# One model step of two trunk layers on one NeuronCore: turning v, k and the output rows in fewer, larger steps

## The chip, the cores and the metric

The kernel runs on one core of a Trainium2 chip. Its time is the device time of one execution in microseconds (us), and the kernel before was run three times. One further execution was recorded by the hardware profiler; the rows quoted below come from that one. Engines are called as the profile calls them: PE is TensorE's matmul side and PEld its weight load, DVE is VectorE, ACT is ScalarE, POOL is GpSimd, and SP is SyncE, which here only issues DMA transfers.

## The reference

One inference step of two layers for a prompt of 512 tokens and 8 samples of one token each, in float32, model width 1024. Layer 0 is a short gated convolution beside dilated sliding-window attention. Layer 1 is mean pooling beside retention in 4 heads of width 256. Each layer has a modulated norm, one wide input and one output projection, and a gated residual. A final RMSNorm gives the output rows. The parts that the change touches:

```python
def retention_chunk(state, q, k, v, log_g):
    ...
    scores = jnp.einsum('bihk,bjhk->bhij', q, k) * decay
    inner = jnp.einsum('bhij,bjhv->bihv', scores, v)
    ...
    kd = k * jnp.exp((L - 1.0 - t)[:, None] * log_g[None, :])[None, :, :, None]
    new_state = jnp.exp(L * log_g)[None, :, None, None] * state + jnp.einsum('bjhk,bjhv->bhkv', kd, v)
    return new_state, inner + cross

def odd_layer(x, c, g, aw, ab, w_in, pw, ps, w_out, pool_prev, ret_prev, pos0):
    ...
    o = o * lax.rsqrt(jnp.mean(o * o, axis=-1, keepdims=True) + EPS)
    y_d = o.reshape(Bn, L, W_D).astype(x.dtype) * jax.nn.silu(gd)
    out = jnp.concatenate([y_c, y_d], axis=-1) @ w_out
    return x + gate * out, pool_new, ret_new.astype(x.dtype)
...
    y_prompt = rmsnorm(xp, norm_f)
    y_sample = rmsnorm(xs, norm_f)
```

The outputs also hold the new retention states of the prompt (one 256x256 per head) and of the 8 samples (8 times as many).

## The kernel before

**Layout.** Activations lie features on partitions, tokens along the free axis: 8 tiles of 128 features by 520 columns (512 prompt tokens and 8 samples). A projection streams weight tiles of 128x1024 from HBM in the fixed order of a list. Float32 products are made of three: each operand is split into a rounded high part and a remainder (fp32r), and hi x hi, hi x lo and lo x hi are summed in PSUM. For weights ACT writes the high part (`whi`) and DVE the remainder (`wlo`).

**The stream.** `product` works on one weight tile in 8 k-steps; each is 6 matmuls (three products by two halves of 260 columns or so). After each k-step `advance` issues the splitting and loading of later weight tiles, and `tick` runs what stands in four lists: `at(n, fn)` runs a function n ticks later; `put(fn, after=n)` puts one into a queue of side steps, of which one runs at each tick once its time has come; `put_fill` steps run where no side step is due; `put2` steps run one at every second tick. So whatever PE does besides projections (transposes, states, scores) stands between two k-steps, and each engine works through its instructions in the order in which these functions wrote them. Semaphores between the engines follow from the tiles.

**Memory.** PSUM holds two 2-bank tiles `mm` for the projections and four 1-bank tiles `aux` for side steps. SBUF has rotating buffers `t` (52 of up to 530 columns), `v` (4 of 1024 columns) and `big` (3 of 2048 columns).

**A retention head** (`ret_head`, four times). Products for v (two tiles), k (two), q (two) and the gate (two) stream by. Beside them run:
- `v_turn` (L970): four transposes of one v tile (L973), so that tokens lie on partitions; ACT writes the high part `vh`, DVE the low one. `v_rows` (L1066, transposes L1069): the 8 samples' v rows are turned, copied by ACT (8x256), written to DRAM (`vdr`) a tick later, and read back spread over all partitions by `v_cast` (tiles `vb`, shown as v).
- `k_turn` (L977, transposes L980): four transposes of one k tile, the decay `kd` by DVE (L146, t<-aux,csm), rounding by ACT, and the remainder by DVE (t<-t,t).
- `state` (four steps): 6 matmuls each of `kd` and `vh`/`vl` (aux<-v,t), the new prompt state.
- `state_new`: for each sample ACT decays the state (big<-big) and DVE adds two outer products (L149, big<-v,ksc,big). It is a `put2` step.
- `score`, `weigh`, `state_read`, `sample_out`, `sample_ms`, `norm`, `gate`: the scores, the weighted sums, the samples' outputs, and the RMS scale of both.

For head 0 the first k-steps run before the layer's normalisation factors are there, so its steps are due later (`DV` = 9 and `DK` = 10 ticks).

**The end.** The last projection goes tile by tile (`out_tile`, 8 of them), `gated` (L149, t<-mm,mG,t) adds the residual, and `rows(m, blocks)` turns a tile's 128 features of a block of 128 tokens (transposes L1299), lets ACT sum the squares, and lets DVE multiply by `norm_f` into output rows. The last tile is done in two column halves. `rows_scale(blocks)` adds the squares, takes the root (ACT) and the reciprocal (DVE, L1308), scales the rows, and sends them (DMA at L1315). Five blocks: four of the prompt and the 8 samples.

## Time and profile before

| what | value |
|---|---|
| three runs | 1062.13, 1062.48, 1064.51 us; median 1062.48 |
| the profiled execution | 1062.29 us |
| its span, first to last instruction | 1060.3 us |
| instructions | 21050 |
| moved by DMA | 168.95 MB, mean 159 GB/s |

The span is shorter than the execution's own time by what lies around it, 2.0 us. The page names groups of instructions by line, engine, operation and tiles: `t<-aux,csm` reads the tiles aux and csm and writes a tile t. L140 is the helper for ACT's activation, L146 DVE's two-tensor operation, L149 the operation of scalar and two tensors, L153 tensor by scalar, L157 a load on SP's queue, L160 every matmul. A row of the timeline has the start in us, the duration of a piece (several instructions of a kind back to back are one row with their count), and in brackets how long the engine was idle before and what ended it. In a row of the windows view stand the window, its length, each engine's busy time, the granted clock, the DMA share and the rate.

The groups of DMA issues in the page show the median from issue to landing:

```profile
wraw<-in_w_in_o SPq DMA_DIRECT2D x48, 512.0 KB, 3.7
big<-in_state_ret SPq DMA_DIRECT2D x16, 512.0 KB, 8.0
```

The weights of layer 1 land 3.7 us after their issue, the samples' states 8.0 us.

### The profile page before, as it was taken

The numbers are of one execution on the slowest core, as the hardware profiler recorded it, in microseconds if no ns is written. First come the engines' busy times: TensorE is split into PE (matmuls) and PEld (weight loads), VectorE is DVE, ScalarE is ACT, GpSimd is POOL, SyncE is SP. The second block draws the span as 40 slices with busy tenths as digits, with TensorE's granted clock in tenths as the row PEclk, the third lists the DMA queues.
The fourth block names the chain that finished last, engine by engine and source line by source line (L and its number), as shares of the span: only waits on it lengthen the run. The fifth ranks groups of instructions, "written<-read, shape, count | busy, mean of one in ns | idle before, by whom it ended". The sixth has DMA issues, their size and how long they took to land.

```text
span 1060.3 us, 21050 instructions
## 1 busy us (share of the span) xinstructions
PE 1036.2 (98%) x8682; PEld 991.1 (93%) x8682; DVE 623.1 (59%) x1470; ACT 489.1 (46%) x884; POOL 4.3 (0%) x33
## 2 busy tenths in 40 slices
PE   5999999999999999999999999999999999999996
PEld 3899999999989999999999998999999999999996
DVE  4666676766785444456344486665657576674443
ACT  5666567665654222224233474435444453333333
POOL 0000000000000000000000000000000000000000
PEclk9999999999999999999999999999999999999999
DMA  9576654666536636613744246363826423225322
GB/s 348 209 255 196 184 157 169 173 211 190 142 119 203 196 107 194 199 60 129 240 154 140 100 159 205 103 204 118 261 83 213 159 80 129 80 83 169 100 71 81
DMA packets 82175, 168.95 MB, mean 159 GB/s; under 512 B 7208, under 2 KB 47240, under 8 KB 79000
## 3 DMA queue, kind: packets, MB, share of 16 engines
q1 hardware_dynamic: 81792, 167.09, 48.9%
q8 instruction: 68, 1.11, 0.4%
q10 hardware_dynamic: 288, 0.52, 0.1%
q14 instruction: 27, 0.22, 0.1%
HBM read 149.40 MB, written 18.65 MB: 158 GB/s over the span
## 4 chain that ended last, share of the span: by engine, by line
PE 90%; DVE 5%; ACT 2%; issue 1%; DVEq 0%; ACTq 0%
PE mm L160 74%; PE aux L160 13%; DVE t L146 2%; PE aux L604 1%; ACT t L140 1%; DVE wlo L146 1%; DVE t L149 0%; PE aux L1299 0%; PE aux L518 0%; DVE big L149 0%; PE aux L973 0%; PE aux L980 0%; PE aux L374 0%; ACT md L140 0%; ACT whi L140 0%
## 5 line engine op out<-in xcount | busy, mean ns | idle before, releaser
L160 PE MATMUL mm<-t,whi 128*128 128x256 f32 (+1 forms) x4608 | 759.1, 286 | 1.1 <-DVE zs L143 0.8
L160 PEld LDWEIGHTS mm<-t,whi 128*128 128x128 f32 x4608 | 636.1, 188 | 19.9 <-issue 15.5
L160 PE MATMUL mm<-t,wlo 128*128 128x256 f32 (+2 forms) x2304 | 465.8, 282 | 0.0
L160 PEld LDWEIGHTS mm<-t,wlo 128*128 128x128 f32 x2304 | 358.1, 188 | 0.0
L146 DVE TENSOR_TENSOR wlo<-wraw,whi 128x512 fp32r<-128x512 f32 x288 | 188.4, 683 | 58.1 <-ACT whi L140 57.4
L140 ACT ACTIVATE whi<-wraw 128x1024 fp32r<-128x1024 f32 x144 | 151.6, 1053 | 94.3 <-PE mm L160 58.7
L146 DVE TENSOR_TENSOR t<-t,t 128x520 fp32r<-128x520 f32 (+6 forms) x182 | 119.0, 657 | 99.3 <-ACT t L140 97.7
L140 ACT ACTIVATE t<-t 128x520 fp32r<-128x520 f32 (+3 forms) x116 | 71.0, 616 | 161.8 <-DVE t L149 103.1
L140 ACT ACTIVATE t<-aux 128x512 f32<-128x512 f32 (+7 forms) x156 | 70.9, 464 | 133.3 <-PE aux L160 83.4
L140 ACT ACTIVATE t<-mm 128x512 f32<-128x512 f32 (+2 forms) x116 | 56.3, 507 | 111.3 <-PE mm L160 109.1
L146 DVE TENSOR_TENSOR t<-aux,t 128x384 fp32r<-128x384 f32 (+6 forms) x120 | 58.6, 494 | 42.8 <-ACT t L140 38.0
L160 PE MATMUL aux<-t,t 64*128 64x256 f32 (+6 forms) x384 | 54.0, 324 | 0.0
L160 PE MATMUL aux<-t,v 128*128 128x512 f32 (+2 forms) x224 | 50.0, 325 | 0.0
L160 PEld LDWEIGHTS aux<-t,t 64*128 64x128 f32 (+1 forms) x384 | 41.0, 186 | 4.3
L583 DVE CUSTOM_DVE_ANT_0 t<-aux,t 128x128 f32<-128x128 f32 (+3 forms) x64 | 28.2, 488 | 27.5 <-PE aux L160 27.5
L140 ACT ACT_TABLE_LOAD x32 | 41.1, 1283 | 1.3 <-PEq L1414 0.7
L140 ACT ACTIVATE t<-t,mn 128x128 f32<-128x128 f32 (+3 forms) x64 | 35.4, 554 | 7.9 <-DVE mn L583 7.9
L160 PEld LDWEIGHTS aux<-t,v 128*128 128x128 f32 x224 | 34.8, 188 | 1.8 <-DVE t L146 0.8
L149 DVE SCALAR_TENSOR_TENSOR big<-v,ksc,big 128x256 f32<-128x256 f32 x64 | 27.7, 480 | 11.8 <-ACT big L140 10.4
L143 DVE COPY zs<-mm 128x8 f32<-128x8 f32 x76 | 12.0, 158 | 37.2 <-ACT t L140 31.8
L146 DVE TENSOR_TENSOR t<-mm,t 128x512 f32<-128x512 f32 (+1 forms) x24 | 16.5, 689 | 29.2 <-PE mm L160 21.6
L146 DVE TENSOR_TENSOR gtmp<-mm,mG 128x8 f32<-128x8 f32 x16 | 2.6, 165 | 44.8 <-PE mm L160 44.8
(153 smaller groups left out, 557.7 us busy)
## 6 DMA issues: line engine op xcount, KB each, us to landing
wraw<-in_w_in_e SPq DMA_DIRECT2D x64, 512.0 KB, 4.9
wraw<-in_w_in_o SPq DMA_DIRECT2D x48, 512.0 KB, 3.7
big<-in_ada_e SPq DMA_DIRECT2D x12, 1024.0 KB, 11.8
big<-in_ada_o SPq DMA_DIRECT2D x12, 1024.0 KB, 9.8
wraw<-in_w_out_e SPq DMA_DIRECT2D x16, 512.0 KB, 3.9
big<-in_state_ret SPq DMA_DIRECT2D x16, 512.0 KB, 8.0
out_new_ret_sample<-big SPq DMA_DIRECT2D x16, 512.0 KB, 5.1
wraw<-in_w_out_o SPq DMA_DIRECT2D x16, 512.0 KB, 3.4
```

What stands on the lines that cost most here:

```text
L140: return nc.scalar.activation(out=out, in_=in_, func=func, scale=scale, **kw)
L143: return nc.vector.tensor_copy(out, in_)
L146: return nc.vector.tensor_tensor(out=out, in0=in0, in1=in1, op=op)
L149: return nc.vector.scalar_tensor_tensor(out=out, in0=in0, scalar=scalar, in1=in1, op0=op0, op1=op1)
L160: nc.tensor.matmul(out, lhsT=lhsT, rhs=rhs, start=start, stop=stop)
L583: nc.vector.tensor_tensor_reduce(out=sb, in0=s[:, 0:n], in1=bt[e][:, S - n:S], scale=1.0, scalar=3e38, op0=ALU.add, op1=ALU.min, accum_out=mn,
L604: nc.tensor.transpose(ep[:, c * P:(c + 1) * P], st["E", e][blk[0]][:, blk[1] * P:(blk[1] + 1) * P], ident)
```

## The change

Layer 0: the transposes and sums of the gate's modulation (`ada_fin` with "g") are no step of their own two ticks after, but the first thing in `window_gather`, four ticks after.

Retention heads: both v tiles and the samples' v rows are turned in one step (10 transposes; before, 4, 4 and 2 in three steps). The 8x256 copy stands first on ACT; the low parts follow one and two ticks later. Both k tiles are turned in one step (8 transposes), the first tile's decay in it, the second's a tick later, the low half of each a tick after its decay (`hilo_later`). The states are due one tick later. The samples' squares are summed over partitions in `norm`, beside the prompt's, and `norm` is due three ticks after `sample_out`, where `sample_ms` was.

The end: the full blocks of `rows` share one PSUM tile; in the stream all five blocks are done in one step, three ticks after (before, three blocks at two ticks and two at four). The output rows lie in two `big` tiles, two blocks each, and one `v` tile for the samples. DVE scales even blocks, ACT odd ones, 1024 columns at a time, and one transfer of 512 KB takes a block out (before, two of 256 KB); odd blocks go by ACT's queue. The samples' rows are one transfer.

```diff
@@ -765,15 +765,15 @@
                         windows[b0 + u][:, t, half * 512:(half + 1) * 512], t == 0, t == 1,
                     )
         mdg = ada_mm(ada_g.pop(b0 // 2))
-        put_fill(ada_fin, 0, "g", b0 // 2, mdg, after=2)
...
-        put(window_gather, b0, om, after=4)
-
-    def window_gather(b0, om):
+        put(window_gather, b0, om, mdg, after=4)
+
+    def window_gather(b0, om, mdg):
+        ada_fin(0, "g", b0 // 2, mdg)
...
@@ -967,20 +967,38 @@
         st = {"of": [], "sq": []}
         yD = [None, None]
 
-        def v_turn(i, vf):
-            pt = aux([P, 4, P])
-            for jb in range(4):
-                nc.tensor.transpose(pt[:, jb, :], vf[:, jb * P:(jb + 1) * P], ident)
-            act(st["vh"][:, :, i, :], pt)
-            lo_of(st["vl"][:, :, i, :], pt, st["vh"][:, :, i, :])
-
-        def k_turn(i, kf):
-            pt = aux([P, 4, P])
-            for jb in range(4):
-                nc.tensor.transpose(pt[:, jb, :], kf[:, jb * P:(jb + 1) * P], ident)
+        def turned(parts):
+            out = []
+            for x in parts:
+                pt = aux([P, 4, P])
+                for jb in range(4):
+                    nc.tensor.transpose(pt[:, jb, :], x[:, jb * P:(jb + 1) * P], ident)
+                out.append(pt)
+            return out
+
+        def v_turn(parts):
+
+            pts = turned(parts)
+            pq = aux([NB, 2, P])
+            for i in range(2):
+                nc.tensor.transpose(pq[:, i, :], zs[1][:, 32 + 2 * h + i, :], ident)
+            vt = tt(2 * P, p=NB)
+            act(vt, flat(pq))
+            at(1, load, vdr[h], vt)
+            at(4, v_cast)
+            for i, pt in enumerate(pts):
+                act(st["vh"][:, :, i, :], pt)
+                at(1 + i, lo_of, st["vl"][:, :, i, :], pt, st["vh"][:, :, i, :])
+
+        def k_turn(parts):
+            pts = turned(parts)
+            k_decay(0, pts[0])
+            at(1, k_decay, 1, pts[1])
+
+        def k_decay(i, pt):
             kd = tt(S)
             vtt(p4(kd), pt, csm[:, C_KDEC + 4 * h:C_KDEC + 4 * h + 4].unsqueeze(2).to_broadcast([P, 4, P]), ALU.mult)
-            st["kd", i] = [p4(x) for x in hilo(kd, S)]
+            st["kd", i] = [p4(x) for x in hilo_later(1, kd, S)]
 
...
@@ -1034,7 +1052,8 @@
                     vtt(st["sq"][0], st["sq"][0], sq, ALU.add)
 
         def norm():
-            ms = aux([P, S])
+            st["om"], ms = aux([P, NB]), aux([P, S])
+            mm(st["om"], on_d, st["oq"][:, 0, :], True, True)
             mm(ms, on_d, st["sq"][0], True, True)
...
@@ -1062,15 +1081,6 @@
         def fin(i):
             yhl[2 * h + i] = hilo(yD[i])
 
-
-        def v_rows():
...
-            at(4, v_cast)
 
...
@@ -1120,17 +1130,13 @@
             vtt(oq, oS, oS, ALU.mult)
             vtt(oq[:, 0, :], oq[:, 0, :], oq[:, 1, :], ALU.add)
             st["oS"], st["oq"] = oS, oq
-            put(sample_ms, after=3)
-
-        def sample_ms():
-            st["om"] = aux([P, NB])
-            mm(st["om"], on_d, st["oq"][:, 0, :], True, True)
             st["orr"] = mk(cp, [P, NB], F32, "orr", 2)
-            put(norm, after=1)
+            put(norm, after=3)
 
 
         st["vh"] = t4(dt=F32R).rearrange("p (a i d) -> p a i d", a=4, i=2)
         st["vl"] = t4(dt=F32R).rearrange("p (a i d) -> p a i d", a=4, i=2)
+        vfs, kfs = [], []
         for i in range(2):
...
-            put(v_turn, i, vf, after=DV if h == 0 else 2)
-        put(v_rows, after=DV if h == 0 else 2)
+            vfs.append(vf)
+        put(v_turn, vfs, after=DV if h == 0 else 2)
         for i in range(2):
...
@@ -1152,12 +1158,13 @@
                 act(p2(kf), ps[:, :, 0:H0], ACTF.Copy, scale=1.0 / 16.0)
                 sample_z(1, 24 + 2 * h + i, ps)
             at(1, k_split, i, kf)
-            put(k_turn, i, kf, after=DK if h == 0 else 2)
+            kfs.append(kf)
+        put(k_turn, kfs, after=DK if h == 0 else 2)
         st["ksc"] = mk(cp, [P, 2, NB], F32, "ksc", 2)
         vts(st["ksc"], zs[1][:, 24 + 2 * h:26 + 2 * h, :], 1.0 / 16.0, None, ALU.mult)
         for i in range(2):
             for part in range(2):
-                put(state, i, part, after=5 + (DK if h == 0 else 0))
+                put(state, i, part, after=6 + (DK if h == 0 else 0))
...
@@ -1274,8 +1281,8 @@
     load(o["pool_keep"], a["state_pool"][0, :, 1:15, :])
 
 
-    xo = [[tt(512) for _ in range(2)] for _ in range(4)]
-    xos = [tt(512, p=NB) for _ in range(2)]
+    xo2 = [big().rearrange("p (i d) -> p i d", i=2) for _ in range(2)]
+    xo = [xo2[i // 2][:, i % 2] for i in range(4)] + [t4(p=NB)]
...
@@ -1293,13 +1300,19 @@
 
         hf, c = m // 4, (m % 4) * P
         sq = tt(P)
+        pts = {}
+        full = [i for i in blocks if i < 4]
+        pt = aux([P, len(full), P])
+        for n, i in enumerate(full):
+            pts[i] = pt[:, n, :]
+        if 4 in blocks:
+            pts[4] = aux([NB, P])
+        for i in blocks:
+            nc.tensor.transpose(pts[i], xT[m][:, i * P:min(i * P + P, T)], ident)
         for i in blocks:
             n = P if i < 4 else NB
-            px = aux([n, P])
-            nc.tensor.transpose(px, xT[m][:, i * P:i * P + n], ident)
-            act(sq[0:n], px, ACTF.Square, scale=1.0 / 32.0, accum_out=ss[0:n, i, m:m + 1])
-            dst = xo[i] if i < 4 else xos
-            vtt(dst[hf][:, c:c + P], px, nf[hf][0:n, c:c + P], ALU.mult)
+            act(sq[0:n], pts[i], ACTF.Square, scale=1.0 / 32.0, accum_out=ss[0:n, i, m:m + 1])
+            vtt(xo[i][:, hf * 512 + c:hf * 512 + c + P], pts[i], nf[hf][0:n, c:c + P], ALU.mult)
 
     def rows_scale(blocks):
         i0, i1 = blocks[0], blocks[-1] + 1
@@ -1307,16 +1320,15 @@
         act(rs[:, i0:i1], rs[:, i0:i1], ACTF.Sqrt, bias=eps[:, 0:1])
         nc.vector.reciprocal(rs[:, i0:i1], rs[:, i0:i1])
         for i in blocks:
-            if i < 4:
-                act(xo[i][0], xo[i][0], ACTF.Copy, scale=rs[:, i:i + 1])
-                vts(xo[i][1], xo[i][1], rs[:, i:i + 1], None, ALU.mult)
-                for hf in range(2):
-                    q = nc.scalar if i == 1 else nc.sync
-                    q.dma_start(out=o["y_prompt"][0, i * P:(i + 1) * P, hf * 512:(hf + 1) * 512], in_=xo[i][hf])
+            if i == 4:
+                vts(xo[i], xo[i], rs[0:NB, i:i + 1], None, ALU.mult)
+                load(o["y_sample"].rearrange("b s d -> (b s) d"), xo[i])
+            elif i % 2:
+                act(xo[i], xo[i], ACTF.Copy, scale=rs[:, i:i + 1])
+                nc.scalar.dma_start(out=o["y_prompt"][0, i * P:(i + 1) * P, :], in_=xo[i])
             else:
-                for hf in range(2):
-                    vts(xos[hf], xos[hf], rs[0:NB, i:i + 1], None, ALU.mult)
-                    load(o["y_sample"].rearrange("b s d -> (b s) d")[:, hf * 512:(hf + 1) * 512], xos[hf])
+                vts(xo[i], xo[i], rs[:, i:i + 1], None, ALU.mult)
+                load(o["y_prompt"][0, i * P:(i + 1) * P, :], xo[i])
 
     def res1(m):
         xT[m] = tt()
@@ -1328,8 +1340,7 @@
         at(6, res1, m + 1)
         out_tile(1, m, ps)
         gated(1, m, ps, xT[m])
-        for n, b in ((2, range(3)), (4, range(3, 5))):
-            at(n if m < KT - 2 else n + 2, rows, m, b)
+        at(3 if m < KT - 2 else 5, rows, m, range(5))
 
 
     m = KT - 1
```

The order of instructions on the engines, at three places. First DVE in head 0, from the decay of the first k tile on. Before, t_7695 is the decayed first k tile and t_7698 its low half; big_7573 is the samples' state that takes up the v rows v_7638; t_7755 is the low half of q; t_7779 and t_7782 are the second k tile.

```order
L146 TENSOR_TENSOR t_7695<-aux_7690,csm 128x512
L146 TENSOR_TENSOR t_7698<-t_7695,t_7697 128x512
L149 SCALAR_TENSOR_TENSOR big_7573<-v_7638,ksc_7662,big_7573 128x256 x2
L146 TENSOR_TENSOR wlo_7716<-wraw_7379,whi_7688 128x512
L149 SCALAR_TENSOR_TENSOR big_7573<-v_7638,ksc_7662,big_7573 128x256 x2
L146 TENSOR_TENSOR wlo_7716<-wraw_7379,whi_7688 128x512
L149 SCALAR_TENSOR_TENSOR big_7573<-v_7638,ksc_7662,big_7573 128x256 x4
L146 TENSOR_TENSOR t_7755<-mm_7671,t_7754 128x512
L143 COPY zs_95<-mm_7671 128x8
L146 TENSOR_TENSOR t_7779<-aux_7774,csm 128x512
L146 TENSOR_TENSOR t_7782<-t_7779,t_7781 128x512
```

After, t_7773 and t_7776 are the first k tile, t_7787 and t_7790 the second, big_7566 the state, t_7744 the low half of q.

```order
L149 SCALAR_TENSOR_TENSOR big_7566<-v_7630,ksc_7662,big_7566 128x256 x2
L146 TENSOR_TENSOR wlo_7705<-wraw_7379,whi_7688 128x512
L149 SCALAR_TENSOR_TENSOR big_7566<-v_7630,ksc_7662,big_7566 128x256 x2
L146 TENSOR_TENSOR wlo_7705<-wraw_7379,whi_7688 128x512
L149 SCALAR_TENSOR_TENSOR big_7566<-v_7630,ksc_7662,big_7566 128x256 x4
L146 TENSOR_TENSOR t_7744<-mm_7671,t_7743 128x512
L143 COPY zs_95<-mm_7671 128x8
L146 TENSOR_TENSOR t_7773<-aux_7763,csm 128x512
L146 TENSOR_TENSOR t_7776<-t_7773,t_7775 128x512
L146 TENSOR_TENSOR t_7787<-aux_7768,csm 128x512
L146 TENSOR_TENSOR wlo_7798<-wraw_7452,whi_7761 128x512
L146 TENSOR_TENSOR t_7790<-t_7787,t_7789 128x512
```

The first k tile's two instructions moved from ahead of the samples' state to behind it, q and the copy to zs; the second k tile follows at once.

Second, DVE in head 1, at the same point. Before, t_8448 and t_8451 are the first k tile and its low half, big_8338 is the samples' state, t_8535 the low half of q.

```order
L146 TENSOR_TENSOR t_8448<-aux_8443,csm 128x512
L146 TENSOR_TENSOR t_8451<-t_8448,t_8450 128x512
L149 SCALAR_TENSOR_TENSOR big_8338<-v_8325,ksc_8415,big_8338 128x256 x2
L146 TENSOR_TENSOR wlo_8469<-wraw_8161,whi_8441 128x512
L149 SCALAR_TENSOR_TENSOR big_8338<-v_8325,ksc_8415,big_8338 128x256 x2
L146 TENSOR_TENSOR wlo_8469<-wraw_8161,whi_8441 128x512
L149 SCALAR_TENSOR_TENSOR big_8338<-v_8325,ksc_8415,big_8338 128x256 x4
L146 TENSOR_TENSOR t_8535<-mm_8424,t_8534 128x512
```

After, t_8442 and t_8445 are the first k tile and its low half, t_8457 and t_8460 the second's.

```order
L146 TENSOR_TENSOR t_8442<-aux_8432,csm 128x512
L149 SCALAR_TENSOR_TENSOR big_8338<-v_8319,ksc_8404,big_8338 128x256 x2
L146 TENSOR_TENSOR t_8445<-t_8442,t_8444 128x512
L146 TENSOR_TENSOR t_8457<-aux_8437,csm 128x512
L146 TENSOR_TENSOR wlo_8468<-wraw_8161,whi_8430 128x512
L146 TENSOR_TENSOR t_8460<-t_8457,t_8459 128x512
L149 SCALAR_TENSOR_TENSOR big_8338<-v_8319,ksc_8404,big_8338 128x256 x2
L146 TENSOR_TENSOR wlo_8468<-wraw_8161,whi_8430 128x512
L149 SCALAR_TENSOR_TENSOR big_8338<-v_8319,ksc_8404,big_8338 128x256 x4
```

Two instructions of the state moved in between the first k tile's decay and its low half, and the second k tile stands ahead of the second pair and among the weights' low halves.

Third, ACT at the end of the program, with what each instruction waits for: the last two blocks. Before, the squares of the two blocks (t_12779), the root, the scaling of the first halves, and block 1's two transfers:

```order
L140 ACTIVATE t_12779,ss<-aux_12780 128x128 [waits PE_49]
L140 ACTIVATE t_12779,ss<-aux_12784 128x128 [waits PE_49,Activation_49]
L140 ACTIVATE rs<-rs,eps 128x2 [waits DVE_49]
L140 ACTIVATE t_11640<-t_11640,rs 128x512 [waits DVE_49]
L140 ACTIVATE t_11642<-t_11642,rs 128x512
L1315 DMA out_y_prompt<-t_11642 128x512 [waits DMAHW7_49,Activation_49]
L1315 DMA out_y_prompt<-t_11643 128x512 [waits DMAHW1_49,DVE_49]
```

After, the squares (t_12737), the root, the scaling of one whole block, and its transfer:

```order
L140 ACTIVATE t_12737,ss<-aux_12738 128x128 [waits PE_49]
L140 ACTIVATE t_12737,ss<-aux_12738 128x128 [waits DVE_49]
L140 ACTIVATE rs<-rs,eps 128x2 [waits DVE_49]
L140 ACTIVATE big_11640<-big_11640,rs 128x1024 [waits DVE_49]
L1328 DMA out_y_prompt<-big_11640 128x1024 [waits DMAHW4_49,Activation_49]
```

Both squares read the same PSUM tile now (aux_12738), and the second waits for DVE, where it waited for PE and for ACT itself.

More of the change, by code (lines that the diff above doesn't have):

```diff
@@ L1063, in fin @@
             yhl[2 * h + i] = hilo(yD[i])
-        def v_rows():
-            pq = aux([NB, 2, P])
-            for i in range(2):
-                nc.tensor.transpose(pq[:, i, :], zs[1][:, 32 + 2 * h + i, :], ident)
-            vt = tt(2 * P, p=NB)
-            act(vt, flat(pq))
-            at(1, load, vdr[h], vt)
-            at(4, v_cast)
         def v_cast():
```

## The prediction

> **What bounds the kernel now.** I read the page's busy line and chain first, then the cores' clocks, then PE's waits.
>
> ```profile
> PE 1036.2 (98%) x8682; PEld 991.1 (93%) x8682; DVE 623.1 (59%) x1470; ACT 489.1 (46%) x884; POOL 4.3 (0%) x33
> PE 90%; DVE 5%; ACT 2%; issue 1%; DVEq 0%; ACTq 0%
> core 0: 1060.3 us, clock 0.998
> PE aux L160 <- DMA t<-in_x_t: 9.2, 1, 9.2
> PE aux L348 <- ACT md L140: 3.4, 2, 1.7
> PE aux L160 <- DVE t L146: 2.0, 4, 1.0
> PE mm L160 <- DVE zs L143: 0.8, 2, 0.7
> ```
>
> TensorE works 98% of the span at full granted clock and makes 90% of the chain. Its waits are few: 9.2 us at the start for the input, then 3.4, 2.0 and 0.8 us. So a change elsewhere can gain only where PE stands today, or at the tail behind PE's last work, and it loses where it makes PE stand. Three things can change: what a group of small PE instructions costs, PE's stalls in the four heads, and the tail.
>
> **Groups of transposes.** A side step slips its PE instructions between two k-steps of six matmuls, two steps become one, and I need the price of a group. The next matmul's start misleads; the price is in the whole gap up to the matmuls behind it.
>
> ```profile
> 613.18 0.41 PE L160 MATMUL mm<-t,wlo 128*128 128x256 f32 x2
> 613.43 0.60 PE L973 MATMUL aux<-csm,t 128*128 128x128 f32 x4
> 614.36 0.41 PE L160 MATMUL mm<-t,wlo 128*128 128x256 f32 x2
> 615.10 0.41 PE L160 MATMUL mm<-t,wlo 128*128 128x256 f32 x2
> 620.72 0.40 PE L160 MATMUL mm<-t,wlo 128*128 128x256 f32 x2
> 620.96 0.38 PE L1069 MATMUL aux<-csm,zs 128*8 128x128 f32 x2
> 621.67 0.41 PE L160 MATMUL mm<-t,wlo 128*128 128x256 f32 x2
> ```
>
> 614.36 to 615.10 is a bare k-step: 0.74 us. With four transposes in it, 613.18 to 614.36 takes 1.18, so they cost 0.44. With two, 620.72 to 621.67 takes 0.95, so they cost 0.21. That is 0.105 to 0.11 each and, from 2 x 0.21 against 0.44, between -0.02 and +0.02 for being a group. The change keeps the number of transposes and ends some 27 groups (two in v and one in k of each head, four sample matmuls in norm, four gathers in layer 0, seven in the output rows). I take 0.008 each, **-0.2 us** (bounds -0.5 and +0.5).
>
> **Head 0.** Here PE does stand today.
>
> ```profile
> 637.26 0.87 PE L160 MATMUL aux<-v,t 128*128 128x256 f32 x6
> 637.97 0.64 PE L160 MATMUL mm<-t,whi 128*128 128x256 f32 x4
> 638.68 0.87 PE L160 MATMUL aux<-v,t 128*128 128x256 f32 x6
> 640.21 0.72 PE L160 MATMUL mm<-t,whi 128*128 128x256 f32 x4 [0.66 <-DVE zs L143]
> 641.38 0.50 PE L160 MATMUL aux<-v,t 128*128 128x256 f32 x2 [0.21 <-ACT t L140]
> 642.11 0.74 PE L160 MATMUL aux<-v,t 128*128 128x256 f32 x4 [0.22 <-DVE t L146]
> 642.68 0.53 PE L160 MATMUL mm<-t,whi 128*128 128x256 f32 x3
> ...
> 631.63 0.68 DVE L146 TENSOR_TENSOR t<-aux,csm 128x512 f32<-128x512 f32 x1
> 633.02 0.69 DVE L146 TENSOR_TENSOR t<-t,t 128x512 fp32r<-128x512 f32 x1 [0.70 <-ACT t L140]
> 634.93 0.88 DVE L149 SCALAR_TENSOR_TENSOR big<-v,ksc,big 128x256 f32<-128x256 f32 x2 [1.22 <-ACT big L140]
> 639.91 0.15 DVE L143 COPY zs<-mm 128x8 f32<-128x8 f32 x1
> 639.99 0.68 DVE L146 TENSOR_TENSOR t<-aux,csm 128x512 f32<-128x512 f32 x1
> 641.36 0.69 DVE L146 TENSOR_TENSOR t<-t,t 128x512 fp32r<-128x512 f32 x1 [0.70 <-ACT t L140]
> ...
> 626.35 0.35 ACT L140 ACTIVATE t<-aux 8x256 f32<-8x256 f32 x1
> 629.10 0.85 SPq L157 DMA_DIRECT2D v<-vdr  x2
> ```
>
> A state step takes 0.71 us (637.26 to 637.97), state plus k-step 1.42. From 638.68 to 642.68 stand two states and a k-step, worth 2.13; it took 4.00, so 1.87 us are lost. The cause is DVE's list: kd0 is decayed at 631.63 and split at 633.02, then DVE waits for the sample state's operands, v rows that return from DRAM (629.10, put on its way by the copy at 626.35), and its pair at 634.93, the rest of that chain, zs and kd1 (639.99) all come late.
>
> In the changed kernel the copy stands first in its step, right behind transposes at about 621: it can come 0 to 5.2 us earlier, I take 2.6. The loads of v rows also stand ahead of a weight load that they followed. kd0 no longer stands ahead of the sample state, so the pair can start as soon as DVE is free, where kd0 was: 631.63, or 3.3 earlier. Then zs ends at 640.06 - 3.3 = 636.8 and the 0.66 wait for it goes. **What is late next** is kd0, now behind that chain: decay to 637.4, rounding on ACT (the 0.70 of idle) to 638.1, split to 638.7. PE reaches the first state one k-step later than now, since it is due a tick later, at 637.97; its third matmul, the first to read the low half, wants it at 638.3. PE stands 0.4, and with restart and rounding I take 0.65. The later states find kd1 ready. Head 0: 0.65 - 1.87 = **-1.2 us**. At best nothing stands, -1.87. If the sample state starts at 634.93 as now, kd0 takes kd1's place (split done 642.05), PE stands 642.05 - 638.3 = 3.75 and some 0.3 for restarts: **+2.2**.
>
> **Heads 1 to 3.** Nothing stands here now; kd0's two parts follow each other with a hole.
>
> ```profile
> 692.20 0.68 DVE L146 TENSOR_TENSOR t<-aux,csm 128x512 f32<-128x512 f32 x1
> 693.58 0.69 DVE L146 TENSOR_TENSOR t<-t,t 128x512 fp32r<-128x512 f32 x1 [0.70 <-ACT t L140]
> 694.19 0.88 DVE L149 SCALAR_TENSOR_TENSOR big<-v,ksc,big 128x256 f32<-128x256 f32 x2
> 691.47 0.60 PE L980 MATMUL aux<-csm,t 128*128 128x128 f32 x4
> 694.05 0.87 PE L160 MATMUL aux<-v,t 128*128 128x256 f32 x6
> ```
>
> The split ends at 694.27; PE's third state matmul reads it at 694.35, hardly spared. The changed order puts the sample pair (0.8 from 692.88, so to about 693.7) into the 0.70 hole. It overfills it by 0.1, and the group of eight transposes moves what stands before kd0, so the split ends some 0.2 behind PE's need: 0.25 a head, **+0.8 us** for three (bounds 0 and +2.3, the latter if the pair still waits half a microsecond for its DMA). The weight splits after it come 1.4 us later (two DVE instructions of 0.69 slipped ahead); no row of PE's waits names a weight, so I cost that at nothing, covered by the tiles split ahead; without that cover it would be 1.4 a head.
>
> **At nothing.** Layer 0's gate sums go two ticks later: read only at that layer's output, many products on. In norm the same two matmuls stand in one step, and its results are read after that head. Output rows in the stream: the same squares and multiplies at three ticks instead of two and four, under PE's products, with DVE 59% and ACT 46% busy. If that cover were gone it would be one block's square and multiply, 0.6 us, in each of seven.
>
> **The tail.**
>
> ```profile
> 1053.12 0.28 ACT L140 ACTIVATE t<-aux 128x128 f32<-128x128 f32 x1
> 1053.12 0.69 DVE L146 TENSOR_TENSOR t<-aux,t 128x128 f32<-128x128 f32 x2 [0.82 <-ACT t L140]
> 1054.46 0.88 DVE L153 TENSOR_SCALAR t<-t,rs 128x512 f32<-128x512 f32 x2
> 1055.20 0.83 SPq L1315 DMA_DIRECT2D out_y_prompt<-t  x2
> 1056.20:1058.70 2.50, 0.00 (x0) 0.00 (x0) 0.00 (x0) 0.00 (x0) 0.00 (x0) 0.50 1.04 394
> ```
>
> Now ACT squares the second block at 1053.12 while DVE multiplies the first: two PSUM tiles. With one tile the changed order makes the second square wait for DVE's first multiply, and the second multiply for that square: +0.35, and +0.11 as the first square waits for both transposes. Then a 1024-wide scaling (0.88 for two halves) comes before the first transfer, which now goes after one 512-wide one: first transfer at 1054.46 + 0.46 + 0.77 = 1055.7 against 1055.20, the second, behind ACT, about when the last goes now. From 1056.20 the transfers run at 394 GB/s, 1 MB in 2.66 us, so they are bound by bytes, and four 256 KB pieces or two of 512 KB differ little: I give back 0.1. **+0.4 us** (bounds -0.1, if the start of the transfers doesn't set their end, and +0.6).
>
> [...]
>
> **The sum.** -0.2 - 1.2 + 0.8 + 0.4 = -0.2. The profiled execution took 1062.29 (span 1060.3), so 1062.1; the median of the three runs, 1062.48, stands 0.19 above it: **1062.3**.
>
> **The rivals.**
> - **Slower: kd0 held behind a transfer.** DVE takes its list in order, and the sample pair now stands ahead of kd0's split in each head, and in head 0 ahead of its decay too. If the pair waits for its v rows, the state step waits with it. Price: head 0 +2.2 in place of -1.2, so 1065.7; with +2.3 in the other heads 1067.2. It decides once the pair in head 0 starts after about 633. For it: that pair waited 1.22 us for its operands today. Against: the copy and loads start earlier.
> - **Faster: no stall left.** Head 0 -1.87, other heads 0, groups -0.2, tail between -0.1 and +0.4: 1060.3 to 1060.8. For it: kd0 misses its turn by only 0.2 to 0.4 in my working.
> - **The change doesn't do what it says, the price being per group.** If ending a group saved a whole 0.1, 27 would give -2.7 and 1059.8. Against: 0.44 for four and 0.21 for two.
> - **The clock falls in the long groups.** The window behind PE's last work shows it at 0.50. Ten transposes take 1.1 us; if each of eight long groups brought 3 us at half speed, 8 x 1.5 = +12, so 1074. Against: that window begins over 3 us after PE stopped, and the mean clock is 0.998 with groups of four and six. [...]
>
> **How the numbers follow.** 0.2% is 2.1 us, about what a measurement of this kernel can tell from no change: faster is below 1060.4, slower above 1064.6. Forecast 0.56 (its own range 1061.0 to 1063.8), slower rival 0.16, faster rival 0.22, per group 0.04, clock 0.02. Of the faster rival half falls below 1060.4: 0.11 + 0.04 = 0.15 faster. Slower: 0.16 + 0.02 less 0.02 where kd0 is held only briefly: 0.16. Within: 0.69. The range takes in the better part of the faster rival and head 0's part of the slower one: 1060.0 to 1066.0.
>
> **What would show it.** Right: PE's row at 640.21 loses its wait for zs, and a short wait for DVE's t stands at the first state of each head; in the tail the two squares of the last tile stand 0.7 apart. Wrong: DVE's pair in head 0 starts at 633 or later and PE's waits for DVE's t grow to 4 us or more; or they vanish in all heads; or k-steps with eight or ten transposes take less than 0.74 + 0.1 for each; or a PEclk below 9 in layer 1.

## The result: slower by 1.3%, and the profile after

| kernel | median us | runs us |
|---|---|---|
| before | 1062.48 | 1061.70 to 1064.51 (5) |
| changed | 1077.48 | 1071.94 to 1079.93 (5) |

The ratio is 1.013, with a 95% interval of 1.0114 to 1.0147. The forecast was 1062.3, and its range ended at 1066.0. The profiled execution took 1079.93 with a span of 1078.0, so it is the slowest of the five and 17.7 us of span above the one before. The five runs' mean clocks go from 0.997 (1071.94) to 0.988 (1079.93).

The changed kernel's page, in the order of before:

```profile
PE 1045.0 (97%) x8682; PEld 998.5 (93%) x8682; DVE 621.9 (58%) x1467; ACT 489.2 (45%) x882; POOL 4.3 (0%) x33
PEclk9999999999999999999999999999899999999998
```

Its span and mean granted clock:

```profile
core 0: 1078.0 us, clock 0.988
```

PE's waits (total us, times, longest):

```profile
PE aux L160 <- DVE t L146: 11.8, 6, 3.9
PE aux L160 <- DMA t<-in_x_t: 8.7, 2, 8.4
PE aux L348 <- ACT md L140: 3.1, 2, 1.7
PE mm L160 <- DVE zs L143: 0.2, 1, 0.2
```

PE does the same 8682 matmuls, but its waits for DVE's t went from 2.0 to 11.8 us, and the clock from 0.998 to 0.988. The wait for zs of head 0 went as forecast. To see where the time came in, I compare the start of the same projection's first matmul in the two traces (later minus earlier, us; before's own times in the first row):

```
                  layer 1  head 1  head 2  head 3  pooling  last matmul
before             597.97  664.39  726.54  788.65   850.73      1051.50
changed             +0.21   -0.87   +5.68  +11.61   +17.78       +17.35
```

Head 0, between "layer 1" and "head 1", gained 1.1 us. Heads 1, 2 and 3 lost 6.55, 5.93 and 6.17, together 18.65, and everything behind them hardly moved. Head 1 on PE, DVE, ACT and SP's queue (start, duration, instruction, idle before):

```profile
693.80 0.40 PE L160 MATMUL aux<-v,t 128*128 128x256 f32 x2
698.06 1.23 PE L160 MATMUL aux<-v,t 128*128 128x256 f32 x4 [3.86 <-DVE t L146]
699.08 1.07 PE L160 MATMUL mm<-t,whi 128*128 128x256 f32 x4
...
690.82 0.69 DVE L146 TENSOR_TENSOR t<-aux,csm 128x512 f32<-128x512 f32 x1
696.52 0.88 DVE L149 SCALAR_TENSOR_TENSOR big<-v,ksc,big 128x256 f32<-128x256 f32 x2 [5.02 <-ACT big L140]
697.32 0.69 DVE L146 TENSOR_TENSOR t<-t,t 128x512 fp32r<-128x512 f32 x1
...
695.86 0.63 ACT L140 ACTIVATE big<-big 128x512 f32<-128x512 f32 x1 [3.69 <-DMA big<-in_state_ret]
...
683.81 0.33 SPq L157 DMA_DIRECT2D wraw<-in_w_in_o  x1
684.23 0.85 SPq L157 DMA_DIRECT2D v<-vdr  x2
685.14 1.06 SPq L157 DMA_DIRECT2D big<-in_state_ret  x2
```

Read it from PE backwards. The first state step starts at 693.80, and its third matmul, which needs kd0's low half, starts at 698.06. That half is made by DVE at 697.32, behind the samples' state pair, which stood 5.02 us. The pair waited for ACT's decay of the state, and that for the load, asked for at 685.14 and landed by 695.86, 10.7 us later. In heads 2 and 3 PE stood 2.97 and 3.18 us at the same place, so 10.0 us in all.

The rest is the clock. Quarter microseconds of the windows view in the changed kernel, with the granted clock third from the end:

```profile
694.50:694.75 0.25, 0.00 (x0) 0.00 (x0) 0.00 (x0) 0.00 (x0) 0.00 (x0) 1.00 0.98 348
696.50:696.75 0.25, 0.00 (x0) 0.00 (x0) 0.23 (x1) 0.00 (x0) 0.00 (x0) 1.00 1.03 332
697.00:697.25 0.25, 0.00 (x0) 0.00 (x0) 0.25 (x2) 0.00 (x0) 0.00 (x0) 0.50 1.10 361
703.50:703.75 0.25, 0.25 (x3) 0.25 (x3) 0.00 (x0) 0.25 (x1) 0.00 (x0) 0.50 0.91 377
704.00:704.25 0.25, 0.25 (x4) 0.25 (x4) 0.25 (x1) 0.00 (x0) 0.00 (x0) 1.00 0.57 209
```

The granted clock fell to 0.50 at about 697, 2.8 us after the last matmul ended (694.2), and came back to 1.00 at about 703.8, though PE worked again from 698.06. A k-step and the state step behind it took 2.58 us there (699.08 to 701.66), against 1.42 in the kernel before (694.76 to 696.18). From the first state step to the k-step behind the third, head 1 took 10.26 us (693.80 to 704.06) against 3.56 before (694.05 to 697.61). That is 6.70 more: the 3.86 of standing and 2.84 behind it. In heads 2 and 3, where the clock was at 0.50 for 6.8 us each and PE worked about 6.2 of them, the same stretch took 9.55 and 9.77 us against 3.59 and 3.55, and 2.99 and 3.04 came behind the standing. So 10.0 of standing and 8.9 behind it make 18.9. (By estimate some 0.8 of the 8.9 is not the clock: in e9 below, where the clock held at 1.00 behind a wait of 3.41, the same stretch of head 1, 695.17 to 702.41, took 0.27 more than 3.56 and the wait.) The merged groups give some 0.3 back (heads 1 to 3 gain 0.26 in e1 and 0.34 in e2 below, where PE does not stand), which makes 18.6 against the 18.65 of the table.

### The profile page after: what moved, and what is told of

The parts are those of the page before. It is cut to its first block, busy times and chain, and to the rows that moved or that the text cites. A ratio compares the mean times of both kernels' runs of the same rounds, so it can differ in the third digit from the quotient of the medians.

```text
span 1078.0 us, 21011 instructions
## 1 busy us (share of the span) xinstructions
PE 1045.0 (97%) x8682; PEld 998.5 (93%) x8682; DVE 621.9 (58%) x1467; ACT 489.2 (45%) x882; POOL 4.3 (0%) x33
## 3 DMA queue, kind: packets, MB, share of 16 engines
q8 instruction: 68, 1.11, 0.4%
q10 hardware_dynamic: 288, 1.05, 0.3%
HBM read 149.40 MB, written 18.65 MB: 156 GB/s over the span
## 4 chain that ended last, share of the span: by engine, by line
PE 84%; DVE 6%; DMA 3%; ACT 3%; issue 1%; SPq 0%; ACTq 0%; DVEq 0%
PE mm L160 68%; PE aux L160 13%; DMA big<-in_state_ret 3%; DVE t L146 2%; ACT t L140 2%; PE aux L604 1%; DVE wlo L146 1%; DVE big L149 1%; DVE t L149 0%; DMA qdr<-t 0%; DVE v L146 0%; PE aux L1311 0%; SPq L157 0%; ACT big L140 0%; ACT whi L140 0%
## 5 line engine op out<-in xcount | busy, mean ns | idle before, releaser
L146 DVE TENSOR_TENSOR t<-aux,t 128x384 fp32r<-128x384 f32 (+4 forms) x80 | 47.2, 598 | 33.4 <-ACT t L140 29.4
L160 PE MATMUL aux<-v,t 128*128 128x256 f32 x96 | 19.8, 351 | 10.1 <-DVE t L146 10.0
```

The lines of the kernel that those rows point to most:

```text
L146: return nc.vector.tensor_tensor(out=out, in0=in0, in1=in1, op=op)
L160: nc.tensor.matmul(out, lhsT=lhsT, rhs=rhs, start=start, stop=stop)
```

## The experiments

Theory A: kd0's low half is held on DVE, which takes its list in order, behind a pair that waits for the state's load; the standing then drops the clock. Rivals: B, the long groups of transposes drop the clock; C, the state steps are due too early whatever DVE does first; D and E, other loads make the state's load late; F, the loads wait in SP's queue. All kernels below are the changed one with one edit, unless said otherwise. Each was timed beside the kernel before on the same chip.

**Both k tiles decayed and split at once (e1).**

```diff
             k_decay(0, pts[0])
-            at(1, k_decay, 1, pts[1])
+            k_decay(1, pts[1])
...
-            st["kd", i] = [p4(x) for x in hilo_later(1, kd, S)]
+            st["kd", i] = [p4(x) for x in hilo(kd, S)]
```

> Both k tiles are decayed and split at once in k_turn, so on DVE both low halves stand ahead of the samples' state pair; transposes, state times and loads stay as changed. Theory A (kd0's split is held on DVE behind a pair that waits for the load of the samples' state): PE's waits for DVE's t in heads 1 to 3 (3.9, 3.0 and 3.2 us in the changed kernel) go, the granted clock stays 1.00 there, about 1061.5 us (before 1062.5, less 1.4 of head 0, plus 0.35 of the tail). Rival B (the long groups of eight and ten transposes drop the clock, not the standing): the clock still falls in heads 1 to 3, some 2.7 us each, about 1069. Rival C (the state steps are due too early whatever DVE does first): waits of 2 us and more stay, 1070 or more.

Measured 1060.46 us, 0.9981 of before (0.9970 to 0.9992). DVE in head 1 of e1:

```profile
693.75 0.69 DVE L146 TENSOR_TENSOR t<-t,t 128x512 fp32r<-128x512 f32 x1 [0.70 <-ACT t L140]
696.45 0.88 DVE L149 SCALAR_TENSOR_TENSOR big<-v,ksc,big 128x256 f32<-128x256 f32 x2 [2.01 <-ACT big L140]
```

PE's waits for DVE's t over the whole of e1:

```profile
PE aux L160 <- DVE t L146: 1.8, 3, 1.0
```

The pair is as late as in the changed kernel (696.45 against 696.52) and DVE still stands 2.01 us for it. But all four k instructions are through by then, PE does not stand, and the mean clock is 0.998 with the same groups of eight and ten transposes. So the late load by itself costs nothing; what stood behind it does. B and C fall. (The time is a microsecond below the expected 1061.5.)

**The pair six ticks later (e2).**

```diff
         for i in range(4):
-            put2(state_new, 0, i)
+            at(6, put2, state_new, 0, i)
```

> The first four state_new steps of each head are put in six ticks later; everything else as changed. Theory A: kd0's split comes right after its rounding, the pair finds its loads landed (about 4 us later than now), PE does not stand: about 1061.5 us. Rival B: clock still falls, about 1069. Rival C: waits stay, 1070 or more.

Measured 1060.28 us, 0.9978 (0.9968 to 0.9987). The same from the other side: the pair moved, the k tiles left as changed.

**The state's load one product earlier (e3).**

```diff
-            if i == 1:
+            if i == 0:
                 state_load(0)
```

> The load of the first half of the samples' state is issued one product (about 6 us) earlier; DVE's order stays as changed, with the pair inside the hole of kd0. Theory A: the load has landed when ACT and DVE come to it, the pair runs in the hole as forecast, PE stands about 0.25 us a head, no clock is lost: about 1062 us. If the pair waits for the v rows and not for the state, nothing changes: about 1077.

Measured 1061.42 us, 0.9985 (0.9976 to 0.9995). DVE's order is the changed one, and of the loads only the state's moved, so it is this load, and not that of the v rows, for which the changed kernel's pair waits in heads 1 to 3. By the table of landmarks these heads lose 0.20, 0.21 and 0.27 us (from -0.85 to -0.17), the 0.25 a head that the prediction had worked out for a load that is there. The pair and kd0's split in head 1 of e3:

```profile
692.73 0.88 DVE L149 SCALAR_TENSOR_TENSOR big<-v,ksc,big 128x256 f32<-128x256 f32 x2 [1.22 <-ACT big L140]
693.53 0.69 DVE L146 TENSOR_TENSOR t<-t,t 128x512 fp32r<-128x512 f32 x1
```

That the size agrees is partly luck. Even with the load there the pair stands 1.22 us, since ACT rounds kd0 first (691.55) and decays the state after that (692.09). So kd0's split starts 1.3 us after its rounding ended (692.2), and not 0.1; PE hardly feels it because kd0's decay had started 1.4 us earlier than in the kernel before (690.83 against 692.20).

**The next loads later (e4).**

```diff
-                state_load(4)
                 st["dec"], st["dec3"] = tt(S), tt(256)
-                load(st["dec"], a["c_dec"][h, :, P:P + S])
-                load(st["dec3"], a["c_dec"][h, :, 0:256])
+                at(6, state_load, 4)
+                at(6, load, st["dec"], a["c_dec"][h, :, P:P + S])
+                at(6, load, st["dec3"], a["c_dec"][h, :, 0:256])
```

> The loads of the second half of the samples' state and of the decay tables (1.4 MB) are issued six ticks later; order on DVE as changed. If these loads share the bandwidth and make the first half land late (theory D, from issues 2.6 us earlier than before), the first half lands about 2 us earlier, PE stands about 1 us a head instead of 3 to 3.9 and the clock holds: about 1065 us. If the first half is late for another reason (its own issue, the v rows ahead of it), the waits stay and so does the time, about 1077.

Measured 1076.0 us, 1.011 (1.0079 to 1.0141). PE stood 3.35, 3.02 and 3.33 us. The state's load was no earlier although 1.4 MB behind it were gone. D falls.

**One weight tile later too (e9).** As e4, and the weight loads of the second k product were written behind that product.

```diff
...
-        if k in (5, 7) and n_raw[0] < n_split[0] + 4:
-            w_raw()
+        if k in (5, 7) and not hold[0]:
+            w_more()
...
+                hold[0] = h > 0
...
+        hold[0] = False
+        at(4, w_more)
         put(k_turn, kfs, after=DK if h == 0 else 2)
```

> As e4 (second half of the state and tables six ticks later), and the weight tile that was issued 0.1 us behind the first half of the state is issued five ticks behind the product too. Theory E (the load of the state shares its 10 us with two weight tiles and the v rows, 3 MB at some 330 GB/s, one of the weight tiles 3 us earlier than in the kernel before): it lands about 1.4 us earlier, PE stands about 2, 1 and 1 us instead of 3.4, 2.9 and 3.1, the clock holds in most runs, about 1066. If the lateness has nothing to do with that tile, as e4: 1076.

Measured 1074.75 us, 1.0108 (1.0093 to 1.0123). PE stood 3.41, 4.04 and 3.04 us. But the edit did not move the tile: SP's queue issued it at 687.68, right behind the state's load (686.52), since nothing made it wait. The run says nothing on E. It shows something of the clock, below.

**v rows asked for one tick earlier (e10).**

```diff
-            at(4, v_cast)
+            at(3, v_cast)
```

> The v rows are asked for one tick earlier, which puts their two loads ahead of a weight tile that SP holds until DVE has split an older one; all else as changed. Theory F (the loads of v rows and state wait in SP's queue behind that weight tile, itself late because the two v tiles' low parts now stand together on DVE): v loads come about 2.5 us earlier, the state's load shares with less and lands 1 to 3 us earlier, PE stands 0.5 to 2.5 us a head and the clock holds: 1063 to 1069 us. If the order on SP doesn't matter: about 1077.

Measured 1061.29 us, 0.9993 (0.9984 to 1.0002). SP's queue, DVE's pair and PE in head 1:

```profile
680.57 0.81 SPq L157 DMA_DIRECT2D v<-vdr  x2
683.42 0.33 SPq L157 DMA_DIRECT2D wraw<-in_w_in_o  x1
683.80 0.98 SPq L157 DMA_DIRECT2D big<-in_state_ret  x2
...
692.47 0.88 DVE L149 SCALAR_TENSOR_TENSOR big<-v,ksc,big 128x256 f32<-128x256 f32 x2 [1.36 <-ACT big L140]
...
694.01 0.74 PE L160 MATMUL aux<-v,t 128*128 128x256 f32 x4 [0.20 <-DVE t L146]
```

The two loads of v rows (1 MB) went ahead of the weight tile that SP holds. The state's load was issued at 683.80, and ACT used it at 691.80 without waiting, so it took at most 8.0 us instead of 10.7, with the other loads still behind it. PE stood 0.20. The time is even below the expected 1063 to 1069, because PE stood less than the 0.5 to 2.5 us foreseen. F holds: which load stood behind the held weight tile decided 2.7 us or more of landing (10.7 against at most 8.0). E stays untested: the weight tile behind the state's load still went out at 685.84 (686.31 in the changed kernel), but 2.0 us behind that load instead of 1.2.

**k apart (e5), v apart (e6).** The old `k_turn` and its states' due time in one, the old `v_turn` and `v_rows` in the other.

```diff
-        put(k_turn, kfs, after=DK if h == 0 else 2)
+            put(k_turn, i, kf, after=DK if h == 0 else 2)
...
-                put(state, i, part, after=6 + (DK if h == 0 else 0))
+                put(state, i, part, after=5 + (DK if h == 0 else 0))
```

> The k tiles are turned apart again, each with its decay and split at once, and the states due as before; v, v rows, norm and the end stay as changed. Theory A: with kd0 done a product earlier, nothing of it stands behind the pair; no wait in heads 1 to 3, clock 1.00, about 1061 us. If the merged v step is what costs (its late low parts, its later loads), waits of PE stay and the time is over 1066.

Measured 1059.25 us, 0.9962 (0.9947 to 0.9977): no wait in the heads, and head 0 gains 1.9 us. A repeat beside e8:

> e5 again, beside e8 on one chip: about 1059.3 to 1060.5 us, that is 0.996 to 0.998 of the kernel before.

gave 1059.66, 0.9973 (0.9962 to 0.9984).

```diff
-        put(v_turn, vfs, after=DV if h == 0 else 2)
+            put(v_turn, i, vf, after=DV if h == 0 else 2)
+        put(v_rows, after=DV if h == 0 else 2)
```

> The v tiles and the v rows are turned in three steps again; k, states, norm and the end stay as changed. Theory A: kd0's split still stands behind the pair, so PE still stands in heads 1 to 3; if the merged v step makes the loads about 1.1 us later, the waits shrink from 3.9, 3.0, 3.2 to about 2 to 3 us each, and the time is 1070 to 1076; without any v effect 1077. If v is the cause, no wait and about 1062.

Measured 1070.95 us, 1.0069 (1.0046 to 1.0092). The time is in the band, but it is made otherwise than expected. PE in head 0 and head 1, and DVE's pair in head 0:

```profile
643.55 1.95 PE L160 MATMUL aux<-v,t 128*128 128x256 f32 x6 [3.40 <-ACT t L140]
703.29 0.74 PE L160 MATMUL aux<-v,t 128*128 128x256 f32 x4 [0.82 <-DVE t L146]
637.11 0.88 DVE L149 SCALAR_TENSOR_TENSOR big<-v,ksc,big 128x256 f32<-128x256 f32 x2 [3.37 <-ACT whi L140]
```

In heads 1 to 3 PE stands only 0.82, 1.09 and 0.87 us, against 3.86, 2.97 and 3.18, so the merged v step brings most of the standing there. In head 0 it is the other way: without the merged v step the pair is late, and both k tiles behind it, so PE stands 3.40 us and the state's six matmuls then take 1.95 instead of 0.87, again at a granted clock of 0.50 (the windows view's figure from 644 on). Here the v rows are what is left for the pair to wait for: ACT had decayed the state by 635.59, the v rows were asked for at 631.12 only, and the pair started at 637.11. That is the case of the prediction's slower rival, which had put 3.75 us of standing on it.

**States two ticks later (e7).**

```diff
-                put(state, i, part, after=6 + (DK if h == 0 else 0))
+                put(state, i, part, after=8 + (DK if h == 0 else 0))
```

> The state steps are due two ticks later (1.4 us of PE), all else as changed. Theory A: PE comes later to the same late split and stands about 2.4, 1.6 and 1.8 us. If the clock falls only after about 3 us without a matmul, it holds here: about 1067 us. If any standing of over a microsecond drops it, 2 to 3 us a head come on top: about 1075.

Measured 1068.07 us, 1.0047 (1.003 to 1.0064). In the profiled run (1065.24, the lowest of four) PE stood 0.74, 1.52 and 1.66 us, and the clock stayed at 1.00 in each of these stretches. The first was expected at 2.4; in head 1 of this run the state's load was also asked for 1.6 us earlier (683.57 against 685.14), and why is open. PE's late matmul in head 3 of e7:

```profile
823.54 0.74 PE L160 MATMUL aux<-v,t 128*128 128x256 f32 x4 [1.66 <-DVE t L146]
```

The same in head 1 of e9:

```profile
698.97 0.74 PE L160 MATMUL aux<-v,t 128*128 128x256 f32 x4 [3.41 <-DVE t L146]
```

And e9's windows view right behind it, with the clock again third from the end:

```profile
699.00:700.00 1.00, 1.00 (x8) 1.00 (x9) 1.00 (x2) 0.45 (x1) 0.00 (x0) 1.00 0.00 0
```

Up to 1.66 us of standing did not cost the clock in the heads of these traces; around 3 us it depended: 2.97 and 3.18 did in the changed kernel, 3.41 did not in e9. The last section shows on what.

**The end with a PSUM tile per block (e8).** As e5, and the last two blocks apart:

```diff
-        pt = aux([P, len(full), P])
-        for n, i in enumerate(full):
-            pts[i] = pt[:, n, :]
+        if len(full) < 4 and 0 in full:
+            for i in full:
+                pts[i] = aux([P, P])
+        else:
+            pt = aux([P, len(full), P])
+            for n, i in enumerate(full):
+                pts[i] = pt[:, n, :]
```

> As e5, and the last tile's two blocks get a PSUM tile each again. If the shared tile costs what the tail rows say (the second square waits for DVE's first multiply), the stretch from the last residual addition to the end of the span is 0.4 us shorter than in e5 and equal to the kernel before; time about 1059, about 0.4 below e5 run beside it.

Measured 1059.07 us, 0.9969 (0.9957 to 0.9980). By the medians that is 0.6 below e5 beside it, but the intervals overlap; the traces are sharper. The tail of the changed kernel:

```profile
1069.18 0.48 DVE L149 SCALAR_TENSOR_TENSOR t<-mm,mG,t 128x256 f32<-128x256 f32 x1 [0.51 <-PE mm L160]
1070.19 0.28 ACT L140 ACTIVATE t<-aux 128x128 f32<-128x128 f32 x1 [1.77 <-PE aux L1311]
1070.92 0.28 ACT L140 ACTIVATE t<-aux 128x128 f32<-128x128 f32 x1 [0.36 <-DVE big L146]
1071.32 0.29 DVE L146 TENSOR_TENSOR big<-aux,t 128x128 f32<-128x128 f32 x1 [0.43 <-ACT t L140]
```

The tail of e8:

```profile
1049.57 0.48 DVE L149 SCALAR_TENSOR_TENSOR t<-mm,mG,t 128x256 f32<-128x256 f32 x1 [0.49 <-PE mm L160]
1050.88 0.28 ACT L140 ACTIVATE t<-aux 128x128 f32<-128x128 f32 x1
1050.88 0.69 DVE L146 TENSOR_TENSOR big<-aux,t 128x128 f32<-128x128 f32 x2 [0.82 <-ACT t L140]
```

With one tile the engines take turns (1070.19, 1070.92, 1071.32); with two they work at once (both at 1050.88). From the last residual addition to the end of the span it is 8.84 us with the shared tile (1078.02 - 1069.18), 8.41 in e8 (1057.98 - 1049.57) and 8.44 before (1060.26 - 1051.82). e8 beats both kernels, the one before by 0.3%: it keeps the rest of the change, the merged v step and the merged norm among it, and leaves k and the last two blocks as they were.

## Why the prediction was wrong, point by point

- **Groups, -0.2: right.** By the median gap around such groups, a step of ten transposes adds 1.09 us to the stream where 4, 4 and 2 added 1.11; eight add 0.87 where two fours added 0.89. That is 0.01 for each group ended, so about -0.3 for 27.
- **Head 0, -1.2: right** at -1.1, by the steps named and with some luck in the size: the copy came early, the pair started at 631.42 (worked out: 631.6), kd0's split at 637.86, the wait for zs is gone.

```profile
631.42 0.88 DVE L149 SCALAR_TENSOR_TENSOR big<-v,ksc,big 128x256 f32<-128x256 f32 x2 [0.32 <-ACT big L140]
637.86 0.69 DVE L146 TENSOR_TENSOR t<-t,t 128x512 fp32r<-128x512 f32 x1 [0.70 <-ACT t L140]
638.14 1.21 PE L160 MATMUL aux<-v,t 128*128 128x256 f32 x6
639.19 0.65 PE L160 MATMUL mm<-t,whi 128*128 128x256 f32 x4
```

The first state step takes 1.05 us to the next matmul instead of 0.71: PE stands 0.34 there, half of the 0.65 worked out. (The sum of the prediction gives 638.8 for the end of this split, not 638.7; it ended at 638.55.) By the gaps around them the four state steps gained 1.5 us. A weighted-sum step at 653.60, of which the prediction says nothing, then took 1.36 us instead of 0.85 and gave 0.5 back.

- **Heads 1 to 3, +0.8 with an end at +2.3: wrong; 18.65.** The step that failed is "it overfills it by 0.1": it took the pair to start at 692.88, as if its operands were there. The bound allowed half a microsecond of waiting; it was 5.02. (The pair's own row has 0.88, so even by its own rows it overfills the hole by 0.2.) The row that left no room was at hand: a state load takes 8.0 us by the page's median. Here are the kernel before's loads and its first use of the state:

```profile
682.75 0.33 SPq L157 DMA_DIRECT2D wraw<-in_w_in_o  x1
683.18 0.86 SPq L157 DMA_DIRECT2D v<-vdr  x2
684.09 1.12 SPq L157 DMA_DIRECT2D big<-in_state_ret  x2
...
693.46 1.66 ACT L140 ACTIVATE big<-big 128x512 f32<-128x512 f32 x3
```

684.09 + 8.0 is 692.1, and with ACT's 0.6 the pair could not start before 692.7 even by that median, 0.2 us ahead of the start that was taken. That no wait was shown there before did not mean room, since ACT came to the state only at 693.46. On top of that the loads moved later against PE: from their issue to the first state step it is 9.96 us before (694.05 - 684.09) and 8.66 now (693.80 - 685.14). The order of SP is the same in both; what moved is when the weight tile ahead of them is let go. It waits for DVE's split of an older tile (which ends at 682.73 before and 683.78 now; the tile is issued at 682.75 and 683.81), and e6 and e10 show that the merged v step and that place in SP's queue make the difference. That it comes from the low parts of the two v tiles standing together on DVE fits the rows, but was not tried by itself.
- **The slower rival: right that kd0 is held behind a transfer, wrong in which one, in place and in price.** It named the v rows; in heads 1 to 3 it was the state's load (e3). It put its 2.2 us on head 0, where the pair started in time (631.42, so its sign, 633 or later, did not show), and 0.77 on each of the others, which lost about 6.
- **The clock rival: right that a fall was possible, wrong in its cause.** It is not the long groups (e1 has them at a mean clock of 0.998); it is PE's standing. No run shows the 3 us at half speed that it put on each long group. I priced the two rivals apart, so the clock stood in the sum at nothing; here the one set off the other, and nearly doubled it: 10.0 became 18.9. The trace before already had a nearer figure than the "over 3 us": PE's last transpose ended at 1052.80, and the clock was at 0.61 in the quarter microsecond from 1055.25, so it fell 2.5 us after.
- **At nothing: right.** Nothing behind the heads loses; from pooling to the last matmul the changed kernel gains 0.4.
- **Tail, +0.4: right.** 8.84 against 8.44, and e8 shows that the shared tile is all of it; one transfer per block costs and gains nothing to be seen.

## What to carry to other kernels

Before moving an instruction that waits for a transfer ahead of others on its engine, find out when the transfer lands, not whether anyone waited for it: a consumer that came later hides that there was no room. Ask it of the whole chain, from the queue that issues the load and what is held ahead of it there. And where a wait of PE may reach some 3 us, price the clock with it: here, by where they fell, waits of 2.97 to 3.86 us cost 2.84 to 3.04 more each (changed kernel, heads 1 to 3), and one of 3.41 only 0.27 (e9, head 1).

## What the runs showed of the hardware

- In these traces the granted clock changed at steps of 3.41 us, and not at a fixed time after the last matmul. In the changed kernel it fell to 0.50 at 696.98, 765.25 and 833.51 and came back at 703.80, 772.07 and 840.34, which is 2, 18, 2, 18 and 2 such steps apart. From the end of the last matmul to the fall it was 2.8, 2.4 and 2.6 us there, and 4.3 in head 2 of e9. Rows of the windows view around the changes, with the clock third from the end; its mean over the quarter microsecond gives the moment:

```profile
765.00:765.25 0.25, 0.00 (x0) 0.00 (x0) 0.25 (x2) 0.00 (x0) 0.00 (x0) 0.99 1.08 344
765.25:765.50 0.25, 0.00 (x0) 0.00 (x0) 0.25 (x1) 0.00 (x0) 0.00 (x0) 0.50 1.09 348
772.00:772.25 0.25, 0.25 (x4) 0.25 (x3) 0.25 (x2) 0.00 (x0) 0.00 (x0) 0.86 0.85 295
833.50:833.75 0.25, 0.00 (x0) 0.00 (x0) 0.25 (x1) 0.00 (x0) 0.00 (x0) 0.52 1.11 360
```

The length of one step is shown by e9, whose clock fell at 765.56 and came back at 768.98:

```profile
765.50:765.75 0.25, 0.25 (x3) 0.25 (x3) 0.25 (x2) 0.00 (x0) 0.00 (x0) 0.62 0.00 0
765.75:766.00 0.25, 0.25 (x3) 0.25 (x3) 0.25 (x2) 0.14 (x1) 0.00 (x0) 0.50 0.00 0
768.75:769.00 0.25, 0.25 (x3) 0.25 (x3) 0.25 (x2) 0.00 (x0) 0.00 (x0) 0.55 0.00 0
769.00:769.25 0.25, 0.25 (x4) 0.25 (x3) 0.25 (x2) 0.00 (x0) 0.00 (x0) 1.00 0.00 0
```

- The falls go by how much of one step PE stood. In the heads of the changed kernel, e4, e6 and e9 the clock fell eight times, each time at the end of a step in which PE had stood 2.24 to 3.13 us. It held wherever no step had more than 1.73: the 3.41 of e9 lay 1.73 in one step and 1.68 in the next. For heads 2 and 3 of e4 the moments are estimates, worked out from the fall in its head 1, the steps and the length of its matmuls. By them it fell in head 2 at 765.43, over a microsecond after PE had started again (764.27): the pair of matmuls at 765.34 took 0.55 us, where the same pair took 0.40 at 760.62. PE need not stand through a whole step: in e4 2.24 of 3.41 us were enough. The clock came back one step later in three of the eight falls and two steps (6.8 us) later in five.
- That the place of a wait in these steps decides fits the spread: the five runs of one kernel differ by 8 us (1071.94 to 1079.93) with mean clocks of 0.997 to 0.988, where the kernel before spreads over 2.8.
- The same 1 MB state load took 10.7 us from issue to use in the changed kernel and at most 8.0 in e10, where the 1 MB of v rows went out 3 us ahead of it instead of 0.9.
